# Four edits around the first layer norm of a streaming encoder step: a bank of its own for one block product, subtractions on VectorE, another order of four tiles, and a later start of the gate rows

## The chip, the core and the metric

The kernel runs on one core of one Trainium2 chip. The metric is device time in microseconds (us). It is one program, launched once, and no part of the arithmetic is done on the host.

## The reference, cut to what matters

One layer works on 576 tokens, 512 of a new stream and 64 of a running one, with a model width of 1024. Everything is float32.

```python
h = layer_norm(ALPHA*x + 0.5*swiglu_ffn(x, ffn1_w_gu, ffn1_w_down), ln1_g, ln1_b)
z = h @ w_in        # mLSTM q,k,v,o,i,f | attention q,k,v | two branch gates
h = layer_norm(ALPHA*h + w_out(sig(g_m)*P_m(mLSTM(z)) + sig(g_a)*P_a(BandAttn(z))), ln2_g, ln2_b)
y = layer_norm(ALPHA*h + 0.5*swiglu_ffn(h, ffn2_w_gu, ffn2_w_down), ln3_g, ln3_b)
```

The change lies at the seam between the first two lines: the end of the first feed-forward network (its down projection), the first norm, and the first products with `w_in`. The layer norm takes mean and variance of each token over the 1024 features. The mLSTM's gates i and f (4 heads each) come out of `w_in` too; a cumulative sum and a running maximum over the tokens make decay weights of them.

## The kernel before, in words

**Numbers and tiles.** Activations lie transposed, features on the 128 partitions and tokens along the free dimension, in 8 tiles of 128x576. A float32 product is made of three fast matmuls: each operand is split into a rounded part ("hi", by an ACT copy) and the rest ("lo", by a DVE subtraction, or by an ACT copy with the sign turned and a DMA from POOL's queue that adds the source to it). The three are hi·hi, hi·lo and lo·hi.

**Products in blocks.** The large products use a seven-product scheme on 2x2 blocks (Strassen and Winograd's): one product is 4 tiles of the inner dimension by 3 matmuls, so 12 matmuls of 128x288. The down projection takes its middle third so, in `seven` (L1115), for the output tiles (0,1), (2,3), (4,5) and, last in the first network, (6,7). `X`, `Y`, `Z` are PSUM banks. `X` collects one product after the other, and between them `ln.take` (L590) adds what stands in `X` to the norm's tiles. A matmul that goes on with `X` must wait until `take` has read it. For the last pair, `first` (L1319) is called inside: there the left token half A of tiles 6 and 7 is complete, and `last` (L600) adds its sums and squares.

**The norm.** `last` leads to `stats` (L648): matmuls with a column of ones give mean and mean square, the reciprocal root is a POOL power, `centre` (L713) subtracts the mean from the eight tiles (tiles 6 and 7 on POOL, the others on DVE, by `CP` at L188), `spread` (L721) brings the scales onto all partitions, and `apply` (L727) scales each tile (DVE), adds the bias (ACT), and splits it into hi (ACT) and lo (DVE). Each half of the tokens goes through this by itself. The halves of the norm are 288 tokens, those of the next product 256 and 320. `centre` serves the second norm and the first half of the third as well.

**The first products with `w_in`.** One `gemm` (L331) makes four tiles: attention v, k and q of the first head pair and the gates i and f (weights 48, 40, 32 and "if"). By `WAVE_M` (L316) the first three take the left half together, tile by tile of the normed activation as it comes, then the fourth the left half; then the same for the right half. The "if" tile has both weight parts packed in one array, so it takes 2 matmuls where the others take 3. There are four PSUM banks of this kind, so the right half's tiles wait for the copies that empty the left half's.

**The units.** `un` (L1709) then runs 12 pairs of tiles of `w_in` by the seven-product scheme, unit after unit. `un.load` brings a pair's raw weights; for every unit DVE makes four sums and the lo parts.

**Order of work.** The order on PE is the order in which the code calls; a clock `od.now` counts matmuls, and `later(d, f)` calls `f` once d of its nanoseconds have gone by. The other engines' rows are placed by a scheduler, by readiness and priority; each engine then runs its rows strictly in the order written. `issue_after` only orders: the step is placed no earlier than another. A planner (`plan`, `pump` at L233) lists all weight blocks in order of use; two raw buffers take turns, SP issues the loads, ACT and DVE split. `PIECES` (L177) names blocks that are split in two halves, `ADDED` (L179) those whose lo part a POOL DMA makes. `gate_rows` (L1375) is a chain of some thirty small steps on 4 partitions, most of them on DVE, handed out one per 1900 of the clock from 50000 after `un.run` has begun (L1760).

Of the kernel before, what the change touches and what calls it, by code (L numbers as in the profile page):

```python
# [14 lines left out]
ALU = mybir.AluOpType  # L15
# [7 lines left out]
KT = D // P  # L23
# [22 lines left out]
class Order:  # L46
# [10 lines left out]
    def later(self, dt, fn):  # L57
        self.seq += 1
        heapq.heappush(self.heap, (self.now + dt, self.seq, fn))
# [29 lines left out]
def tile_layer(ctx: ExitStack, tc: tile.TileContext, ins, outs):  # L89
# [64 lines left out]
    def stt(out, a, s, b, op0, op1):  # L154
        return DVE.scalar_tensor_tensor(out=out, in0=a, scalar=s, in1=b, op0=op0, op1=op1)  # L155
# [9 lines left out]
    def blank(out, like, behind=None):  # L165
# [8 lines left out]
    CL = {1: 2, 2: 3}  # L174
    NX, NX_IN = 10, 11
    NH0, NH1 = 1, 6
    PIECES = {("in", 48), ("in", 40), ("in", 32)}  # L177

    ADDED = {("in", c + j) for c in (32, 40, 48) for j in range(2, KT)} | {("in", c) for c in (*range(2, 8), *range(10, 32), *range(56, 72))} \  # L179
        | {("gu2", 1, 1), ("gu2", 2, 0), ("gu2", 2, 1)}  # L180

    HALVED = {("in", c + j) for c in (32, 40) for j in range(3, KT)}
# [2 lines left out]

    EARLY = [("gu2", 0, 0), ("gu2", 0, 1), ("gu2", 1, 0)]
    EARLY1 = [("in", 16), ("in", 17)]
    CP = (6, 7)  # L188
    GR = 1900
    L_MEAN, L_STATS, L_SPREAD, L_SPREAD1 = 300, 1440, 4920, 2600  # L190
    plan = []
# [190 lines left out]
    def plan_ffn(n):  # L382
        for j in range(CL[n]):
            for e in range(2):
                plan.append(((f"gu{n}", j, e), ins[f"w_gu{n}"][e * FT + j]))
        stops.append(len(plan))

        def chunk(j, c):
            k0, nk = DC[c]
            plan.append(((f"dn{n}", j, c), ins[f"w_dn{n}"][j][:, k0 * P:(k0 + nk) * P]))  # L390

        def seven(j, order="uv"):
            for e, x in enumerate("at"):
                plan.append(((f"ds{n}", j, x), ins[f"w_dn{n}"][j + e][:, KT * P:2 * KT * P]))
            for x in order:
                plan.append(((f"ds{n}", j, x), None))

        for j, c in ((1, 0), (3, 0), (1, 2), (3, 2), (5, 0), (5, 2)):
            chunk(j, c)
        for j in (0, 2, 4):  # L400
            seven(j)
            chunk(j, 0)
            chunk(j, 2)
        if n == 1:
            for j in (6, 7):
                chunk(j, 0)
                chunk(j, 2)
            seven(6, "vu")
            chunk(6, 0)
            chunk(6, 2)  # L410
            return
        for r in range(2):
            for j in (6, 7):
                for c in range(3):
                    chunk(j, c)

    def plan_in(cols_):
        for c in cols_:
            plan.append((("in", c), w_in[c]))

    plan_ffn(1)
    plan_in((48, 40, 32))
    plan.append(("if", ins["w_if"]))
    plan_in((16, 17))
    stops.append(len(plan))
    for j in range(1, KT):
# [688 lines left out]
    def seven(n, j, inner, ln, Y=None, first=None):  # L1115

        ids = {}
        at = {"a11": ("a", 512), "a12": ("a", 0), "t0": ("t", 512), "t1": ("t", 0), "q1": ("u", 512), "a22": ("u", 0),
              "q0": ("v", 0)}

        def product(ps, what, xk, start, end=None):
            w_, c0 = at[what]
            for w in "atuv" if first is None else "atvu":
                if w_ not in ids and w not in ids:
                    ids[w] = take((f"ds{n}", j, w))
            wh, wl = parts[ids[w_]]
            for i in range(4):
                ww = slice(c0 + i * P, c0 + (i + 1) * P)
                xh, xl = inner.b[i][xk]
                for w, x in ((wh, xh), (wh, xl), (wl, xh)):  # L1130
                    mm(ps, w[:, ww], x, start and i == 0 and w is wh and x is xh, False, skip_group_check=True)
                od.tick()
            if end:
                done(ids[end])

        X, Z = bank("mm")[:, :HT_], bank("mm")[:, :HT_]
        new = Y is None
        if new:
            Y = bank()[:, :HT_]
        product(X, "a11", "b11", True)  # L1140
        ln.take(j, A, X, ALU.add)
        product(Y, "a12", "b21", new, "a")
        product(X, "t0", "t2", False)
        ln.take(j, B, X, ALU.add)
        if first is None:
            product(Z, "q1", "t1", True)
            ln.take(j + 1, B, Z, ALU.subtract)
        product(X, "q0", "t3", False, "v")
        ln.take(j + 1, B, X, ALU.subtract)
        if first is None:  # L1150
            product(Z, "t1", "b22", False, "t")
        product(X, "a22", "t4", False, "u" if first is None else None)
        ln.take(j + 1, A, X, ALU.subtract)
        if first is not None:
            first()
            product(Z, "q1", "t1", True, "u")
            ln.take(j + 1, B, Z, ALU.subtract)
            product(Z, "t1", "b22", False, "t")
        return Y, Z

# [212 lines left out]
            stt(hs(dst, hf), hs(dst, hf), scol[:, bc:bc + 1], hs(tmp, hf), ALU.add, ALU.add)  # L1373

    def gate_rows():  # L1375
        yield stt(t1, fx, -1.0, fx, ALU.mult, ALU.max)
        yield act(t1, t1, AF.Exp, scale=-1.0)
        yield ts(t2, t1, 2.0, None, ALU.add)
        for a in range(0, T, 144):
            yield DVE.reciprocal(t2[:, a:a + 144], t2[:, a:a + 144])  # L1380
        yield tt(t1, t1, t2, ALU.mult)
        yield tt(t2, t1, t1, ALU.mult)
        yield ts(t3, t2, 1.0 / 15, None, ALU.mult)
        for c in (13, 11, 9, 7, 5, 3):
            yield stt(t3, t3, 1.0 / c, t2, ALU.add, ALU.mult)
        yield stt(t3, t3, 1.0, t1, ALU.add, ALU.mult)
        yield ts(t3, t3, 2.0, None, ALU.mult)
        yield stt(t3, fx, 0.0, t3, ALU.min, ALU.subtract)
        bcum, arow, mt = t2, t1, t3
        for a, b in ((0, NP_), (NP_, T)):  # L1390
            yield DVE.tensor_tensor_scan(out=bcum[:, a:b], data0=z4.to_broadcast([4, b - a]), data1=t3[:, a:b], initial=0.0,
                                         op0=ALU.add, op1=ALU.add)
        yield tt(arow, li, bcum, ALU.subtract)
        yield DVE.tensor_tensor_scan(out=mrow[:, :NP_], data0=z4.to_broadcast([4, NP_]), data1=arow[:, :NP_], initial=0.0,
                                     op0=ALU.add, op1=ALU.max)
        yield DVE.tensor_tensor_scan(out=mrow[:, NP_:], data0=z4.to_broadcast([4, NS]), data1=arow[:, NP_:],
                                     initial=scol[:, 2:3], op0=ALU.add, op1=ALU.max)
        yield tt(mt, bcum, mrow, ALU.add)
        SP.dma_start(outs["m"][:, 0:1], mt[:, NP_ - 1:NP_])
        SP.dma_start(outs["m"][:, 1:2], mt[:, T - 1:T])  # L1400
        for i, (a, b) in enumerate(((0, NP_), (NP_, T))):
            ts(scol[:, 4 + i:5 + i], mrow[:, b - 1:b], -1.0, None, ALU.mult)
            yield act(rows[32:36, a:b], arow[:, a:b], AF.Exp, bias=scol[:, 4 + i:5 + i])

        yield ts(rows[32:36, :], rows[32:36, :], 1.0 / 16, None, ALU.mult)
        yield act(rows[64:68, :], mt, AF.Exp, scale=-1.0)
        yield act(wd[:, 0:64], mrow[:, NP_:], AF.Exp, bias=scol[:, 2:3], scale=-1.0)
        yield act(wd[:, 64:65], mrow[:, T - 1:T], AF.Exp, bias=scol[:, 2:3], scale=-1.0)

        yield act(mr[0:64, :], mw)  # L1410
        yield tt(mr[32:36, :], mw[0:4, :], f(mr[0:4, :]), ALU.subtract)
        yield None
        for b in range(5):
            w = min(P, T - b * P)
            ps = bank()
            transpose(ps[:w, :P], rows[:, b * P:b * P + w], ident)
            yield DVE.tensor_copy(tcol[:w, b, :].rearrange("p (g h) -> p g h", h=4),
                                  ps[:w, :96].rearrange("p (g r) -> p g r", r=32)[:, :, 0:4])
        gdone.append(1)
        yield None  # L1420
# [9 lines left out]
    def out_cb(t, key, j):  # L1430
        def cb(hf, ps):
            with tc.issue_after(k0a[0].ins) if j == 1 and key == "v" else nullcontext():
                act(hs(t, hf), ps)
            if hf == 1:
                SP.dma_start(outs[key][:, j, :], t)
        return cb
# [265 lines left out]
    def keep_g(c, tiles):  # L1702
        for e in range(2):
# [5 lines left out]
    un = Columns([(b + c, b + c + 1) for c, b in pairs],  # L1709
                 [lambda tiles, c=c, fn=KEEP[b]: fn(c, tiles) for c, b in pairs],  # L1710
                 stp, None, cw, combos)
    un.load(0)
    un.load(1)
    for i, key in enumerate(EARLY1):
        later(9000 + 4000 * i, lambda key=key: early(e1, key, EARLY1))
    gemm([[(("in", 48), KT)], [(("in", 40), KT)], [(("in", 32), KT)], [("if", KT)]], H,
         [out_cb(vf0, "v", 0), out_cb(kf0, "k", 0), q0_cb, gate_cb], WAVE_M)
    wst["ahead"] = 2
    for i in range(4):
        combos.last = combos.add(i)  # L1720
# [9 lines left out]
    with tc.tile_pool(name="cx", bufs=1, side="right", reuse_waits="tile") as cx:  # L1730
# [26 lines left out]
            wst["stop"] = stops[0]  # L1757
            pump(2)

        later(50000, lambda: od.bg.append((GR, gate_rows())))  # L1760
        un.run(tail)
    pstack.close()
    opool.append(ostack.enter_context(tc.tile_pool(name="op", bufs=8, reuse_waits="tile")))
# [563 lines left out]
```

## Time and profile before

| | |
|---|---|
| runs, us | 1553.64, 1553.24, 1552.8 |
| median, us | 1553.24 |
| profiled execution, us | 1553.24 |
| its span, first to last instruction, us | 1551.5 |
| outside the span, us | 1.74 |
| PE busy, us | 1530.7 |
| mean granted TensorE clock | 0.998 |

Stretches below are given in us from the span's start. The first network's down projection ends near 394, the four tiles of `w_in` run to 424.7, two more tiles of `w_in` to 437.5, and the units from there to about 575.

In the views, a row of the timeline gives start, duration, engine, source line, operation, output<-input, and how many instructions it merges; in brackets stands how long the engine had been idle before it and which engine and tile ended that. Tiles are named without their numbers: `s` is any tile of the pool "slots" (norm tiles and hi and lo parts among them), `st` a unit's tile, `wr` and `wu` raw weights, `wh` and `wl` their hi and lo parts, `mm` and `aux` PSUM banks. Line 135 is the helper for every matmul, 149 for an ACT copy, 152 and 155 for DVE's two tensor forms.

### The profile page before, as it was taken

What the parts mean: (1) busy time and instruction counts of PE and PEld (TensorE: products, weight loads), DVE (VectorE), ACT (ScalarE), POOL (GpSimd) and SP (SyncE); (2) the same over time, 40 slices, a digit from 0 to 9 for tenths busy, and PEclk for the clock granted to TensorE, in tenths of its full rate; (3) what the DMA queues carried; (4) which work ended last, traced back from release to release, by engine and by line L of the source; (5) the groups of instructions that cost most, each with busy time, mean ns of one, the idle gap of its engine ahead of it and who ended that gap; (6) DMA issues with size and microseconds to landing.
All of it is one profiled execution on the core that took longest, in us unless ns stands there. A gap on an engine that the chain in (4) does not pass through costs nothing.

```text
span 1551.5 us, 29498 instructions
## 1 busy us (share of the span) xinstructions
PE 1530.7 (99%) x11579; PEld 1516.1 (98%) x11579; DVE 1140.2 (73%) x2103; ACT 891.7 (57%) x1700; POOL 234.7 (15%) x437
## 2 busy tenths in 40 slices
PE   9999999999999999999999999999999999999998
PEld 9999999999899999999999999999999999999997
DVE  7877778675988766777586766755776877788756
ACT  7544457442866557777754877753456454457333
POOL 1000000000310015555311222202121000001000
PEclk9999999999999999999999999999999999999999
DMA  9232323533754438687534765642755323226334
GB/s 262 108 109 83 105 86 93 142 108 89 204 150 155 137 130 223 153 204 188 120 137 137 189 145 138 163 144 82 210 141 128 109 82 109 82 72 145 119 113 150
DMA packets 80260, 211.15 MB, mean 136 GB/s; under 512 B 9081, under 2 KB 20985, under 8 KB 80121
## 3 DMA queue, kind: packets, MB, share of 16 engines
q1 hardware_dynamic: 65144, 169.15, 33.3%
q0 software_dynamic: 11808, 34.28, 12.7%
q10 hardware_dynamic: 3168, 5.83, 1.1%
q8 instruction: 91, 1.49, 0.4%
q14 instruction: 49, 0.39, 0.1%
HBM read 172.27 MB, written 21.63 MB: 125 GB/s over the span
## 4 chain that ended last, share of the span: by engine, by line
PE 87%; DVE 4%; ACT 4%; DMA 2%; POOL 1%; issue 1%; SPq 0%; ACTq 0%; DVEq 0%; POOLq 0%
PE mm L135 70%; PE aux L135 15%; PE aux L145 2%; DVE s L152 1%; ACT sc L149 1%; DVE wl L152 1%; DVE sc L1585 1%; DMA s<-in_xT 1%; ACT s L149 1%; DMA G<-in_rbias 1%; ACT wh L149 0%; POOL kh L159 0%; DMA wr<-in_w_gu 0%; ACT wh L872 0%; DVE s L155 0%
## 5 line engine op out<-in xcount | busy, mean ns | idle before, releaser
L135 PE MATMUL mm<-s,wh 128*128 128x288 f32 (+2 forms) x3667 | 752.2, 298 | 6.9 <-DVE s L152 3.1
L135 PEld LDWEIGHTS mm<-s,wh 128*128 128x128 f32 x3667 | 588.0, 189 | 11.4 <-DVE s L152 2.3
L135 PE MATMUL mm<-s,wl 128*128 128x288 f32 (+2 forms) x1806 | 533.1, 295 | 0.0
L135 PEld LDWEIGHTS mm<-s,wl 128*128 128x128 f32 x1806 | 340.0, 188 | 0.0
L149 ACT ACTIVATE wh<-wr 128x1024 fp32r<-128x1024 f32 (+2 forms) x143 | 134.0, 948 | 156.7 <-PE mm L135 91.3
L152 DVE TENSOR_TENSOR wl<-wr,wh 128x1024 fp32r<-128x1024 f32 (+2 forms) x93 | 107.5, 1164 | 49.0 <-ACT wh L149 48.6
L135 PE MATMUL mm<-tx,wh 128*128 128x288 f32 x677 | 140.3, 296 | 0.8 <-DVE tx L152 0.8
L135 PEld LDWEIGHTS mm<-tx,wh 128*128 128x128 f32 x677 | 109.2, 188 | 1.2 <-DVE tx L152 1.0
L152 DVE TENSOR_TENSOR wl<-wt,wh 128x1024 fp32r<-128x1024 f32 x51 | 62.5, 1225 | 55.8 <-ACT wh L872 55.8
L135 PE MATMUL mm<-tx,wl 128*128 128x288 f32 x350 | 103.2, 295 | 0.0
L872 ACT ACTIVATE wh<-wt 128x1024 fp32r<-128x1024 f32 x51 | 54.1, 1060 | 83.1 <-DVE wt L152 83.1
L152 DVE TENSOR_TENSOR wl<-wu,wh 128x1024 fp32r<-128x1024 f32 x63 | 77.1, 1223 | 31.3 <-ACT wh L872 31.3
L872 ACT ACTIVATE wh<-wu 128x1024 fp32r<-128x1024 f32 x63 | 66.7, 1058 | 41.2 <-PE mm L135 34.3
L135 PE MATMUL mm<-tx,ah 128*128 128x288 f32 x416 | 85.4, 297 | 0.4 <-ACT st L149 0.4
L198 POOL DMA_DIRECT2D s<-s x16 | 13.7, 854 | 469.4 <-DVE hb L152 426.7
L149 ACT ACTIVATE h<-h 128x288 f32<-128x288 f32 x78 | 34.0, 436 | 60.9 <-DVE h L152 60.9
L135 PEld LDWEIGHTS mm<-tx,ah 128*128 128x128 f32 x416 | 66.2, 188 | 1.2 <-ACT st L149 0.6
L135 PEld LDWEIGHTS mm<-tx,wl 128*128 128x128 f32 x350 | 65.7, 188 | 0.0
L152 DVE TENSOR_TENSOR ws<-wu 128x1024 f32<-128x1024 f32 (+1 forms) x55 | 64.7, 1176 | 0.0
L152 DVE TENSOR_TENSOR wl<-ws,wh 128x1024 fp32r<-128x1024 f32 x51 | 62.2, 1219 | 3.0 <-ACT wh L872 3.0
L135 PE MATMUL mm<-h,wh 128*128 128x288 f32 (+2 forms) x304 | 62.7, 296 | 0.1
L135 PE MATMUL mm<-tx,al 128*128 128x288 f32 x208 | 61.1, 294 | 0.0
(398 smaller groups left out, 3481.8 us busy)
## 6 DMA issues: line engine op xcount, KB each, us to landing
wu<-in_w_gu SPq DMA_DIRECT2D x78, 512.0 KB, 4.4
wr<-in_w_in SPq DMA_DIRECT2D x48, 512.0 KB, 4.2
wr<-in_w_dn SPq DMA_DIRECT2D x37, 512.0 KB, 3.8
wl<-in_w_in POOLq DMA_DIRECT2D x36, 512.0 KB, 6.3
wu<-in_w_in SPq DMA_DIRECT2D x24, 512.0 KB, 4.5
wr<-in_w_dn SPq DMA_DIRECT2D x19, 384.0 KB, 3.2
s<-s POOLq DMA_DIRECT2D x16, 288.0 KB, 4.4
wu<-in_w_ap SPq DMA_DIRECT2D x8, 512.0 KB, 4.7
```

The lines of the kernel that those rows point to most:

```text
L135: PE.matmul(out, lhsT, rhs, start=start, stop=stop, **kw)
L145: PE.transpose(out, in_, idn)
L149: return ACT.activation(out, in_, func, **kw)
L152: return (eng or DVE).tensor_tensor(out, a, b, op=op)
L198: return POOL.dma_start(lo, src, accum_op=ALU.add)
L872: self.last = ACT.activation(hi, src, AF.Copy)
L1585: DVE.tensor_tensor_reduce(out=out, in0=ps, in1=g, op0=ALU.add, op1=ALU.min, scale=1.0, scalar=3e38, accum_out=acc)
```

## The change

1. In `seven`, for the last pair (6,7) only, the product of `q1` and `t1` (into `Z`) comes before that of `q0` and `t3`, and the last product into `X` (`a22` by `t4`) goes to a bank `R` of its own, which `take` reads separately. The planner's order of the two blocks "v" and "u" goes back to "u", "v".
2. `CP` is empty: `centre` subtracts on DVE alone, in all norms.
3. The `gemm` of four tiles takes v, k, "if" and, as the fourth, q. The block ("in", 32) of q is loaded after "if", is split in one piece, and gets its lo part by a POOL DMA. The first two `un.load` are called 8000 and 10500 after this point on the clock.
4. `gate_rows` is handed out from 30000 on, and its first step is placed after the lo part of the unit that was prepared last.

```diff
-    PIECES = {("in", 48), ("in", 40), ("in", 32)}
+    PIECES = {("in", 48), ("in", 40)}
...
-    ADDED = {("in", c + j) for c in (32, 40, 48) for j in range(2, KT)} | {("in", c) for c in (*range(2, 8), *range(10, 32), *range(56, 72))} \
+    ADDED = {("in", 32)} | {("in", c + j) for c in (32, 40, 48) for j in range(2, KT)} | {("in", c) for c in (*range(2, 8), *range(10, 32), *range(56, 72))} \
...
-    CP = (6, 7)
+    CP = ()
...
-            seven(6, "vu")
+            seven(6)
...
-    plan_in((48, 40, 32))
+    plan_in((48, 40))
     plan.append(("if", ins["w_if"]))
+    plan_in((32,))
...
-            for w in "atuv" if first is None else "atvu":
+            for w in "atuv":
...
-        if first is None:
-            product(Z, "q1", "t1", True)
-            ln.take(j + 1, B, Z, ALU.subtract)
+        product(Z, "q1", "t1", True)
+        ln.take(j + 1, B, Z, ALU.subtract)
         product(X, "q0", "t3", False, "v")
         ln.take(j + 1, B, X, ALU.subtract)
         if first is None:
             product(Z, "t1", "b22", False, "t")
-        product(X, "a22", "t4", False, "u" if first is None else None)
-        ln.take(j + 1, A, X, ALU.subtract)
-        if first is not None:
+            product(X, "a22", "t4", False, "u")
+            ln.take(j + 1, A, X, ALU.subtract)
+        else:
+            R = bank()[:, :HT_]
+            ln.take(j + 1, A, X, ALU.subtract)
+            product(R, "a22", "t4", True, "u")
+            ln.take(j + 1, A, R, ALU.subtract)
             first()
-            product(Z, "q1", "t1", True, "u")
-            ln.take(j + 1, B, Z, ALU.subtract)
             product(Z, "t1", "b22", False, "t")
...
     def gate_rows():
-        yield stt(t1, fx, -1.0, fx, ALU.mult, ALU.max)
+        with tc.issue_after(un.lo.ins):
+            first = stt(t1, fx, -1.0, fx, ALU.mult, ALU.max)
+        yield first
...
-    un.load(0)
-    un.load(1)
+    for i in range(2):
+        later(8000 + 2500 * i, lambda i=i: un.load(i))
...
-    gemm([[(("in", 48), KT)], [(("in", 40), KT)], [(("in", 32), KT)], [("if", KT)]], H,
-         [out_cb(vf0, "v", 0), out_cb(kf0, "k", 0), q0_cb, gate_cb], WAVE_M)
+    gemm([[(("in", 48), KT)], [(("in", 40), KT)], [("if", KT)], [(("in", 32), KT)]], H,
+         [out_cb(vf0, "v", 0), out_cb(kf0, "k", 0), gate_cb, q0_cb], WAVE_M)
...
-        later(50000, lambda: od.bg.append((GR, gate_rows())))
+        later(30000, lambda: od.bg.append((GR, gate_rows())))
```

Three places show how the rows move. First DVE, while PE makes the last products of the pair (6,7). `s_3591` is tile 7 of the norm and `s_3589` tile 6, `mm_4342` is the bank `X`, `mm_4343` is `Z`, `aux_4420` the new bank `R`; `s_430` and `s_431` are the sums and the sums of squares; `wl` rows split weights. Before:

```order
L152 TENSOR_TENSOR s_3589<-s_3589,mm_4342 128x288
L152 TENSOR_TENSOR s_431_3035<-s_431_3035,sq_4427 128x288
L152 TENSOR_TENSOR s_3591<-s_3591,mm_4342 128x288
L152 TENSOR_TENSOR wl_4411<-wr_4351,wh_4410 128x768
L152 TENSOR_TENSOR s_3591<-s_3591,mm_4342 128x288
L152 TENSOR_TENSOR s_430_3034<-s_430_3034,s_3591 128x288
L152 TENSOR_TENSOR s_431_3035<-s_431_3035,sq_4431 128x288
L152 TENSOR_TENSOR s_3591<-s_3591,mm_4343 128x288
```

Now:

```order
L152 TENSOR_TENSOR s_3589<-s_3589,mm_4342 128x288
L152 TENSOR_TENSOR s_431_3035<-s_431_3035,sq_4442 128x288
L152 TENSOR_TENSOR s_3591<-s_3591,mm_4343 128x288
L152 TENSOR_TENSOR s_3591<-s_3591,mm_4342 128x288 x2
L152 TENSOR_TENSOR s_430_3034<-s_430_3034,s_3591 128x288
L152 TENSOR_TENSOR wl_4426<-wr_4351,wh_4425 128x768
L152 TENSOR_TENSOR s_3591<-s_3591,aux_4420 128x288
L152 TENSOR_TENSOR wl_4489<-wr_4395,wh_4488 128x512
L152 TENSOR_TENSOR s_430_3034<-s_430_3034,s_3591 128x288
L152 TENSOR_TENSOR s_431_3035<-s_431_3035,sq_4446 128x288
```

The read of `Z` has moved up, the two reads of `X` stand together, the read of `R` is an added row, and between it and the reads of `X` stand a sum of the right half and the split of a weight block of 768 columns; half a `w_in` block is split ahead of the two sums of the left half.

Second ACT, in the left half of the norm. `s_3042` and `s_3036` are the first two norm tiles (bias rows), `s_4523`, `s_4538` (now `s_4537`, `s_4555`) their hi parts, `sq` a square. Before:

```order
L149 ACTIVATE wh_4503<-wr_4414 128x512 x2
L149 ACTIVATE wh_4549<-wr_4501 128x512 x2
L149 ACTIVATE s_3042<-s_3042,cols 128x288
L149 ACTIVATE s_3036<-s_3036,cols 128x288
L149 ACTIVATE s_4523<-s_3042 128x288
L149 ACTIVATE wh_4679<-wr_4509 128x8x64
L149 ACTIVATE s_3585<-s_3585,cols 128x288
L149 ACTIVATE sq_4589<-s_3589 128x288
L149 ACTIVATE s_4538<-s_3036 128x288
```

Now:

```order
L149 ACTIVATE wh_4496<-wr_4429 128x512 x2
L149 ACTIVATE wh_4545<-wr_4494 128x8x64
L149 ACTIVATE s_3042<-s_3042,cols 128x288
L149 ACTIVATE s_3036<-s_3036,cols 128x288
L149 ACTIVATE sq_4576<-s_3589 128x288
L149 ACTIVATE s_4537<-s_3042 128x288
L149 ACTIVATE wh_4660<-wr_4502 128x1024
L149 ACTIVATE s_4555<-s_3036 128x288
L149 ACTIVATE wl_4661<-wh_4660 128x1024
L149 ACTIVATE s_3585<-s_3585,cols 128x288
```

The block of q (`wr_4501` before, `wr_4502` now) has moved from ahead of the norm's rows to between the hi parts of the first and the second tile, as one row of 1024, and a second row of 1024 (`wl_4661`) is new.

Third DVE, in the second unit (`ws_5229`, now `ws_5230`, are its weight sums); `t_4611`, `t_4612` and `rows` belong to the gate rows. Before:

```order
L152 TENSOR_TENSOR ws_5229<-wu_4672 128x1024
L159 TENSOR_SCALAR t_4611<-rows 4x576
L152 TENSOR_TENSOR wt_5230<-ws_5229,wu_4672 128x512
L1380 RECIPROCAL t_4611<-t_4611 4x144
L152 TENSOR_TENSOR wt_5230<-wt_5230,wu_4672 128x512
L1380 RECIPROCAL t_4611<-t_4611 4x144 x3
L152 TENSOR_TENSOR st_5172<-mm_5187,st_5172 128x288
L152 TENSOR_TENSOR wl_5248<-wt_5230,wh_5247 128x1024
L152 TENSOR_TENSOR rows<-rows,t_4611 4x576
L152 TENSOR_TENSOR t_4611<-rows 4x576
L159 TENSOR_SCALAR t_4612<-t_4611 4x576
L155 SCALAR_TENSOR_TENSOR t_4612<-t_4612,t_4611 4x576 x4
```

Now:

```order
L152 TENSOR_TENSOR ws_5230<-wu_4839 128x1024
L152 TENSOR_TENSOR wt_5231<-ws_5230,wu_4839 128x512
L152 TENSOR_TENSOR wt_5231<-wt_5231,wu_4839 128x512
L152 TENSOR_TENSOR st_5173<-mm_5188,st_5173 128x288
L152 TENSOR_TENSOR wl_5249<-wt_5231,wh_5248 128x1024
L152 TENSOR_TENSOR wl_5280<-ws_5230,wh_5279 128x1024
L155 SCALAR_TENSOR_TENSOR st_5174<-st_5174,mm_5252 128x288
```

The gate rows have left the second unit; the first of them now stands in the fourth unit and the last in the ninth, one or two at a time between the units' own. On SP, the first load of a unit's weights now stands ahead of the load of q's block.

## The prediction

> **What bounds the kernel now.** I read the page first, then the waits of PE, then PE's timeline at each wait, then the other engines' timelines there.
>
> ```profile
> span 1551.5 us, 29498 instructions
> PE 1530.7 (99%) x11579; PEld 1516.1 (98%) x11579; DVE 1140.2 (73%) x2103; ACT 891.7 (57%) x1700; POOL 234.7 (15%) x437
> ```
>
> PE works for 1530.7 of 1551.5 us. The change removes no matmul, so it can only move PE's 20.8 idle us. The waits of PE (total, times, longest) name the candidates:
>
> ```profile
> PE mm L135 <- DVE s L152: 3.3, 5, 1.2
> PE mm L135 <- ACT vf L149: 1.5, 1, 1.5
> PE mm L135 <- DVE st L155: 1.4, 1, 1.4
> PE mm L135 <- ACT st L149: 0.4, 1, 0.4
> ```
>
> They add up to 6.6 us, the most that this change could win here. PE's timeline shows where they lie:
>
> ```profile
> 379.06 0.50 PE L135 MATMUL mm<-s,wh 128*128 128x288 f32 x2 [1.21 <-DVE s L152]
> 381.53 0.50 PE L135 MATMUL mm<-s,wh 128*128 128x288 f32 x2 [0.64 <-DVE s L152]
> ...
> 384.79 1.39 PE L135 MATMUL aux<-onec,s 128*128 128x1 f32 x12
> ...
> 395.91 0.39 PE L135 MATMUL mm<-s,wh 128*128 128x256 f32 x1 [1.07 <-DVE s L152]
> ...
> 407.91 2.08 PE L135 MATMUL mm<-s,wh 128*128 128x256 f32 x16
> 411.52 0.56 PE L135 MATMUL mm<-s,wh 128*128 128x320 f32 x2 [1.53 <-ACT vf L149]
> ...
> 424.69 0.40 PE L135 MATMUL mm<-s,eh 128*128 128x256 f32 x2
> ...
> 451.83 0.53 PE L135 MATMUL mm<-s,wh 128*128 128x288 f32 x2 [1.44 <-DVE st L155]
> ...
> 482.72 0.53 PE L135 MATMUL mm<-tx,ah 128*128 128x288 f32 x2 [0.40 <-ACT st L149]
> ```
>
> 379.06 and 381.53 are the waits for `take` to read `X`; 384.79 is the left half's statistics; 395.91 the first normed tile; 407.91 the fourth tile's left half; 411.52 the right half, waiting for v's bank; 424.69 the end of the four tiles; the last two lie in the units. So the seam is ruled by a chain through DVE and ACT, not by PE. What counts is when that chain delivers.
>
> **Part 1, the own bank.** It removes 1.21 + 0.64 = 1.85 us of waiting. From 381.53 to 384.79 PE made two products, so one takes 1.6. Without the waits, from 377.7 on: `Z`, `X`, `R` and `Z` again, four products, end at 384.1, `R` at 382.5. But the statistics need sums that DVE makes:
>
> ```profile
> 381.73 0.96 DVE L152 TENSOR_TENSOR wl<-wr,wh 128x768 fp32r<-128x768 f32 x1 [0.34 <-ACT wh L149]
> 383.40 0.45 DVE L152 TENSOR_TENSOR s<-s,mm 128x288 f32<-128x288 f32 x1 [0.71 <-PE mm L135]
> ...
> 384.37 0.46 DVE L152 TENSOR_TENSOR s<-s,sq 128x288 f32<-128x288 f32 x1
> 385.56 0.69 DVE L152 TENSOR_TENSOR wl<-wr,wh 128x512 fp32r<-128x512 f32 x1
> ```
>
> In the new order, once `X` is done at 381.1, come two reads of `X` and a sum (3 x 0.45), the split of 768 columns (0.96), the read of `R` (0.45), half a block (0.6 net of overlap), and the two sums (0.9): 385.1, with the first sum at 384.75. Before, the last of these ended at 384.83. PE, ready at 384.1, waits some 0.75 and begins the statistics at 384.85, the old 384.79. So nothing is won yet, and 12 matmuls that used to follow the statistics now precede them: PE gets through what hides the norm (42 matmuls, 5.6 us, with 1.6 of statistics and 0.3 more) at 392.3.
>
> **Part 2, subtractions on DVE.** From the means to the first tile:
>
> ```profile
> 387.55 1.43 DVE L152 TENSOR_TENSOR s<-s,c 128x288 f32<-128x288 f32 x2
> 389.00 0.97 DVE L152 TENSOR_TENSOR s<-s,sq 128x288 f32<-128x288 f32 x1
> 389.89 1.28 DVE L152 TENSOR_TENSOR wl<-wr,wh 128x512 fp32r<-128x512 f32 x2
> 391.09 1.55 DVE L152 TENSOR_TENSOR s<-s,c 128x288 f32<-128x288 f32 x4
> 392.57 0.93 DVE L155 SCALAR_TENSOR_TENSOR s<-s,cols,aux 128x288 f32<-128x288 f32 x2
> ...
> 395.41 0.81 DVE L152 TENSOR_TENSOR s<-s,s 128x288 fp32r<-128x288 f32 x2
> ...
> 399.43 0.68 DVE L152 TENSOR_TENSOR wh<-wr,wh 128x512 fp32r<-128x512 f32 x1
> ```
>
> ```profile
> 386.81 0.41 ACT L149 ACTIVATE c<-aux 128x288 f32<-128x288 f32 x1
> ...
> 388.54 0.43 ACT L149 ACTIVATE sq<-s 128x288 f32<-128x288 f32 x1
> 388.87 1.14 ACT L149 ACTIVATE wh<-wr 128x512 fp32r<-128x512 f32 x2
> ```
>
> ```profile
> 387.68 1.98 POOL L152 TENSOR_TENSOR s<-s,c 128x288 f32<-128x288 f32 x2
> ...
> 395.46 2.46 POOL L159 TENSOR_SCALAR mr<-rows 64x576 fp32r<-64x576 f32 x2
> ```
>
> Four subtractions alone took 1.55, so about 0.37 each; beside POOL's two, two took 1.43 and a sum 0.97 instead of 0.45. POOL's part cost DVE 1.2 us; on DVE the two cost 0.74, a gain of 0.45 a half. The new order spends it: two subtractions from 387.2, a wait until ACT has the square (388.5, one root row ahead of it where three were), the sum, two more, the two half blocks from 389.66 (ACT's pair at 388.87 releases them), four more, and the "if" split (0.68), which stood at 399.43. That gives 392.95 for the first scaling, against 392.57. Then bias, square and hi on ACT: the first lo part ends at 395.8, against the old release at 395.91. So PE, there at 392.3, waits 3.5: the 1.85 is spent. The second and third norm have PE covered by other products; I take 0, with 0.3 either way.
>
> [...] POOL's 2.46 us of `mr` reads SBUF while DVE subtracts at 395.41, and DVE's rows there are not stretched (0.81 for two). [...]
>
> **Part 3, q as the fourth tile.** Its block's load must wait for the raw buffer that the 40 block leaves at 390.9, and ACT reaches the block's row at 395.15, just ahead of the second tile's hi part. Loads of one `w_in` block around there, alone and behind four unit loads (KB, us to landing):
>
> ```profile
> wr<-in_w_in SPq DMA_DIRECT2D x1, 512.0 KB, 3.8
> ...
> wr<-in_w_in SPq DMA_DIRECT2D x1, 512.0 KB, 6.9
> ```
>
> The first unit load was issued here, the start and length of two on SP's queue:
>
> ```profile
> 391.58 1.42 SPq L864 DMA_DIRECT2D wu<-in_w_in  x2
> ```
>
> Now one unit load is in front of it on SP's queue; I take 4.2, nearer the lower, so 395.25: no loss yet, with 2.7 us more at the upper end. ACT then spends 1.04 on hi, and as much on the sign-turned copy (`el` is the same step of another block, `c` the right half's mean, `vf` the copy that empties v's bank):
>
> ```profile
> 402.02 0.39 ACT L149 ACTIVATE c<-aux 128x288 f32<-128x288 f32 x1
> ...
> 405.54 1.04 ACT L149 ACTIVATE el<-eh 128x1024 fp32r<-128x1024 f32 x1
> ...
> 411.11 0.36 ACT L149 ACTIVATE vf<-mm 128x256 f32<-128x256 f32 x1
> ```
>
> So the second tile's lo part comes at 397.1 and PE loses 0.4 there, and as much again twice where ACT's hi parts come late. The right half's mean, which ended at 402.4, stands three ACT rows of about 0.43 later, at 403.7; then all eight subtractions and the seventh tile's lo (9 x 0.37) run ahead of the eighth tile's lo, which ends at 407.45. PE does that tile by 408.4, then q's 24 matmuls (2.9, by 16 in 2.08): 411.3, where before it was at 410.0. One more copy of 1.04 stands ahead of ACT's right half, and one norm row (0.45) less between that and v's copy, so v's bank is emptied at 412.1 instead of 411.47: +0.6. Six matmuls (0.9) later PE needs the "if" bank, behind the copies of k and four more (5 x 0.36): 413.9, another 0.95 of waiting, where before q's bank cost 0.15. Sum of parts 1 to 3 at 424.69: 0.6 + 0.95 - 0.15 = **+1.4** (0 to +4.1). The unit loads are needed only in the units, after the four tiles and two more: hidden.
>
> **Part 4, gate rows.** DVE between 440 and 452:
>
> ```profile
> 440.93 2.85 DVE L1380 RECIPROCAL t<-t 4x144 f32<-4x144 f32 x3
> ...
> 447.19 3.09 DVE L155 SCALAR_TENSOR_TENSOR t<-t,t 4x576 f32<-4x576 f32 x4
> ...
> 451.34 0.43 DVE L155 SCALAR_TENSOR_TENSOR st<-st,mm 128x288 f32<-128x288 f32 x1
> ```
>
> The last row releases PE at 451.83; 5.94 us of gate rows stand in the 11 before it. It needs an ACT copy of a product that ended at 447, so without them it is ready at 448, before PE needs it (450.4). The 0.40 at 482.72 is the same queue. Gone: **-1.84**. In their new place the rows fill DVE's slack of some 3 us in a unit of seven products (11.1); my count has one unit over by 1.3, within the 1.9 that PE allows. I take **+0.2** (0 to 1.3).
>
> Sum: 1.4 - 1.84 + 0.2 = -0.24. The profiled execution took 1553.24, equal to the median, with 1.74 outside its span: **1553.0**.
>
> **The rivals.** (a) *The chain gives way*: scheduled rows run closer, or the sums come as soon as PE is done, so the 1.85 is kept, v's wait (1.53) vanishes behind q's 24 matmuls, and the gate rows' 1.84 with them: 1548.0. For it: all three waits are in the rows; against it: DVE's queue as counted. (b) *Slower, by q's load*: if the unit load in front of it is let go only at the end of the down projection (392.3), SP issues q's block at about 392.7 or later; at 6.9 us it lands at 399.6 and ACT, stopped at 395.15, gives the second tile 4.4 us late: 1557.4. It decides from a landing after 395.2; it is over 0.2% slower from 398.6 on. For it: SP's queue is strict; against it: the buffer of that unit load was free by 391.58 before. (c) *Gate rows were not the cause*: the units' own DVE rows are late, +1.4 stays, 1554.6. [...]
>
> **How the numbers follow.** A measurement of this kernel can tell about 0.2% (3.1 us) from no change. Forecast with its bounds 0.56, (a) 0.15, (b) 0.13, (c) 0.12, (d) 0.04. Faster by over 0.2% (under 1550.1) takes (a): 0.15. Slower (over 1556.3) takes most of (b): 0.11. Within: 0.74. The range reaches down to half of what (a) adds and up past (c), (d) and the load's upper end (1553.0 + 2.7): 1550.3 to 1556.0.
>
> **What would show it.** Right: no wait at the two `X` products; a new wait of about 0.75 at the statistics; 3 us or more before the first `w_in` matmul; the right half starting near 412 with a wait at the "if" bank; 426 for the end of the four tiles; no wait near 452. Wrong: the four tiles end before 424.7, or PE waits over 1 us in the units, or ACT stands at q's block after 396.

## The result, and the profile after

| | before | after |
|---|---|---|
| median of 19 runs, us | 1553.71 | 1555.92 |
| lowest and highest | 1552.39, 1555.94 | 1553.59, 1557.91 |
| ratio after/before | | 1.0015, 95% interval 1.0008 to 1.0021 |
| profiled execution and its span, us | 1553.24, 1551.5 | 1557.87, 1556.2 |
| PE busy, us | 1530.7 | 1537.2 |
| mean granted clock | 0.998 (profiled), 0.998 or 0.999 in 120 later runs | 0.997 or less in 18 of 19 runs |

The change costs 2.2 us, where the forecast was a gain of 0.24. The time lies within the range and within the 0.2% that were called no change, but the interval excludes no change. The profiled execution lies near the upper end of the 19, so its rows show more of the loss than the medians do. One reason lies outside the seam: near its end, from 1529.0 to 1532.75, the clock was down for another 3.42 us.

The page of the kernel after, its first part and the clock by slices:

```profile
span 1556.2 us, 29491 instructions
PE 1537.2 (99%) x11579; PEld 1523.1 (98%) x11579; DVE 1137.7 (73%) x2112; ACT 893.5 (57%) x1701; POOL 226.1 (15%) x428
...
PEclk9999999999899999999999999999999999999999
```

PE is busy 6.5 us longer with the same 11579 matmuls. It doesn't only wait; it works more slowly. The one 8 in the last row is the slice from 389 to 428. The windows there (PE, PEld, DVE, ACT, POOL busy with instructions, then granted clock, DMA share, GB/s) before:

```profile
390.00:394.00 4.00, 4.00 (x30) 3.90 (x29) 4.00 (x9) 2.06 (x6) 0.03 (x1) 1.00 0.53 136
394.00:396.00 2.00, 0.92 (x6) 0.48 (x4) 2.00 (x6) 1.82 (x6) 1.86 (x4) 1.00 0.95 346
396.00:398.00 2.00, 2.00 (x18) 2.00 (x18) 2.00 (x6) 1.23 (x4) 1.88 (x3) 1.00 1.00 381
...
404.00:406.00 2.00, 1.83 (x15) 1.62 (x15) 2.00 (x6) 2.00 (x5) 0.27 (x1) 1.00 0.00 0
```

and after:

```profile
390.00:394.00 4.00, 3.53 (x25) 3.19 (x24) 4.00 (x10) 1.18 (x3) 0.94 (x2) 1.00 0.58 190
394.00:396.00 2.00, 0.29 (x1) 0.19 (x1) 2.00 (x6) 1.63 (x4) 1.78 (x4) 1.00 1.04 361
396.00:398.00 2.00, 1.72 (x8) 1.57 (x7) 1.29 (x4) 1.24 (x2) 0.55 (x2) 0.50 0.96 299
...
404.00:406.00 2.00, 2.00 (x11) 2.00 (x10) 0.73 (x2) 2.00 (x7) 0.00 (x0) 0.50 0.34 64
406.00:408.00 2.00, 2.00 (x16) 1.91 (x15) 1.64 (x5) 2.00 (x5) 0.00 (x0) 0.94 0.00 0
```

From 396.0 to 406.2 the granted clock is 0.50, summed over quarter microseconds for 10.24 us. At half the clock that makes 5.1 us more of PE's busy time, and the 3.42 near the end 1.7. In the 2 us ahead of 396, PE has done 0.29 us of work. PE's timeline after:

```profile
385.39 1.47 PE L135 MATMUL aux<-onec,s 128*128 128x1 f32 x12 [0.38 <-DVE s L152]
...
395.71 0.38 PE L135 MATMUL mm<-s,wh 128*128 128x256 f32 x1 [2.19 <-ACT s L149]
396.37 0.58 PE L135 MATMUL mm<-s,wh 128*128 128x256 f32 x1 [0.28 <-DVE s L152]
...
399.93 2.55 PE L135 MATMUL aux<-onec,s 128*128 128x1 f32 x12
...
415.01 0.56 PE L135 MATMUL mm<-s,wh 128*128 128x320 f32 x2 [0.48 <-ACT vf L149]
416.72 0.85 PE L135 MATMUL mm<-s,wh 128*128 128x320 f32 x4 [0.56 <-ACT t L149]
...
428.85 0.40 PE L135 MATMUL mm<-s,eh 128*128 128x256 f32 x2
```

The two waits at `X` are gone. In their place stands one wait of 2.19 ahead of the hi part of the first normed tile, and 0.28 ahead of its lo part. In the kernel before, PE didn't wait for the hi part, and the 1.07 was for the lo part:

```profile
394.46 0.38 PE L135 MATMUL mm<-s,wh 128*128 128x256 f32 x1
```

After the wait the statistics of the right half, the same twelve matmuls as at 385.39, take 2.55 us, since the clock is halved. To compare stretches I set each profile's zero at DVE's read of an `aux` bank near 373, before and after:

```profile
372.75 0.45 DVE L152 TENSOR_TENSOR s<-s,aux 128x288 f32<-128x288 f32 x1 [3.08 <-PE aux L135]
```

```profile
373.53 0.46 DVE L152 TENSOR_TENSOR s<-s,aux 128x288 f32<-128x288 f32 x1 [2.13 <-PE aux L135]
```

From there to the first `eh` matmul, the end of the four tiles, it was 51.94 us (424.69 - 372.75) and is 55.32: the seam is 3.38 longer. I call this the seam below. In the units the wait of 1.44 is gone.

A second thing shows on SP's and ACT's timelines after: a unit's load goes out ahead of q's block, and ACT stands 1.10 us at that block.

```profile
389.88 0.33 SPq L865 DMA_DIRECT2D wu<-in_w_in  x1
391.52 0.33 SPq L252 DMA_DIRECT2D wr<-in_w_in  x1
```

```profile
396.76 1.06 ACT L149 ACTIVATE wh<-wr 128x1024 fp32r<-128x1024 f32 x1 [1.10 <-DMA wr<-in_w_in]
397.73 0.43 ACT L149 ACTIVATE s<-s 128x288 fp32r<-128x288 f32 x1
```

So there were two theories. **A**: the long wait lets the granted clock fall, and that is the loss. **B**: q's block is late, ACT gives the second tile's hi part (397.73) late, and the rest follows.

### The profile page after: what moved, and what is told of

Read it like the earlier page. It is cut to its first block, busy times and chain, and to the rows that moved or that the text cites. A ratio compares the mean times of both kernels' runs of the same rounds, so it can differ in the third digit from the quotient of the medians.

```text
span 1556.2 us, 29491 instructions
## 1 busy us (share of the span) xinstructions
PE 1537.2 (99%) x11579; PEld 1523.1 (98%) x11579; DVE 1137.7 (73%) x2112; ACT 893.5 (57%) x1701; POOL 226.1 (15%) x428
## 4 chain that ended last, share of the span: by engine, by line
PE 87%; ACT 4%; DVE 4%; DMA 2%; issue 1%; POOL 1%; DVEq 0%; POOLq 0%; ACTq 0%
PE mm L135 70%; PE aux L135 15%; PE aux L145 2%; DMA G<-in_rbias 1%; ACT sc L149 1%; DVE sc L1589 1%; ACT wh L149 1%; ACT wh L873 1%; ACT s L149 1%; DVE wl L152 1%; DMA og<-od 0%; DMA wr<-in_w_in 0%; POOL kh L159 0%; DVE kl L152 0%; DVE ptl L152 0%
```

## The experiments

All times are medians of 11 runs beside the kernel before on the same chip. "Low clock" counts the runs with a mean granted clock of 0.997 or less; the kernel before had 0 of 120 such runs in all. The count is coarse. In the profiles before and after the clock is also down in the last 4.6 and 3.1 us, and one fall of 3.4 us takes only 1.7 off 1551, about 0.001, so a mean of 0.998 doesn't rule one out: the profiles of e9_q_first and e12_part2 have 0.998 and such a fall at the seam. (20 of the 120 runs of the kernel before have 0.998.) The seam's difference is from one profile each.

| run | us | to before, us | ratio, 95% interval | low clock | seam |
|---|---|---|---|---|---|
| e1_fill16 | 1555.20 | +1.21 | 0.9996 to 1.0014 | 7 of 11 | +0.96 |
| e2_no_part1 | 1554.45 | +0.46 | 0.9995 to 1.0013 | 8 of 11 | +1.47 |
| e3_no_part3 | 1556.78 | +2.79 | 1.0008 to 1.0025 | 9 of 11 | +4.28 |
| e4_part4 | 1553.03 | -0.96 | 0.9987 to 1.0005 | 0 of 11 | +0.01 |
| e5_fill512x10 | 1555.21 | +1.33 | 0.9996 to 1.0013 | 5 of 11 | +2.81 |
| e6_fill128x4 | 1555.98 | +2.10 | 1.0000 to 1.0018 | 10 of 11 | +3.41 |
| e7_part1 | 1556.05 | +2.17 | 1.0003 to 1.0021 | 8 of 11 | +2.02 |
| e8_part3 | 1552.15 | -1.73 | 0.9976 to 0.9994 | 0 of 11 | -1.44 |
| e9_q_first | 1554.18 | +0.17 | 0.9992 to 1.0010 | 4 of 11 | +1.48 |
| e10_q_first_fill | 1552.64 | -1.37 | 0.9982 to 1.0000 | 0 of 11 | +0.47 |
| e11_parts34 | 1552.25 | -1.76 | 0.9979 to 0.9996 | 0 of 11 | -1.41 |
| e12_part2 | 1556.06 | +2.05 | 1.0004 to 1.0021 | 4 of 11 | +3.29 |
| e13_part1_fill | 1553.77 | -0.33 | 0.9989 to 1.0007 | 0 of 11 | +0.34 |
| e14_parts134_fill | 1553.34 | -0.76 | 0.9985 to 1.0003 | 0 of 11 | -0.25 |

**e1_fill16**, spare matmuls in PE's wait of the changed kernel:

```diff
 o = pss[t, hf][:, :HALVES[hf][1]]
+for _ in range(fill):     # 16 at the first tile of the four-tile gemm
+    PE.matmul(o[:, 0:P], ones_r, ones_r, start=True, stop=True)
+fill = 0
```

> The changed kernel with 16 spare matmuls of 128 columns (ones by ones, overwritten by the first real one) put into TensorE's wait ahead of the first normed tile's product; they compute nothing of the output. Theory A (the 2.2 us wait lets the granted clock fall to 0.50 for 10.2 us, and that is the loss): the wait shrinks to about 0.5, the clock stays 1.00 from 390 to 410, the right half's statistics take 1.4 again instead of 2.55, mean clock 0.998, time about 1553.6, that is 2.3 below the changed kernel. Theory B (q's block lands late and ACT stands at it, the clock is a by-product): the time stays at 1555.5 to 1556 whatever the clock does.

Neither, cleanly. In the profiled execution the clock stayed up and the statistics took 1.39 again, but 7 of 11 runs still had a low clock. The three runs at 0.999 took 1552.06, 1552.80 and 1553.75; the seven low ones took 1554.91 to 1555.65. In these ten the time goes with the clock, from run to run of one and the same kernel. The eleventh, at 0.998, was the slowest, 1556.98; its cause is open. What brought the clock down was not removed in all of them.

**e2_no_part1, e3_no_part3, e4_part4**: the change without part 1, the change without part 3, and part 4 alone; their code is that of the diff above.

> Parts 2, 3 and 4 without part 1 (the last product in X's bank again). Theory A: the two waits at X are back (1.2 and 0.6), so PE comes later to the first normed tile and waits at most 1.5 in one piece there; the clock stays 1.00, mean 0.998; part 3 costs its 1.4 and part 4 gives 1.6: about 1553.5. Theory B: q's load is as late as before, ACT stands 1.1 at it: 1555.5 with a clock that doesn't fall.

> Parts 1, 2 and 4 without part 3 (q third, split into pieces as before). Theory A: the wait ahead of the first normed tile is still 2 us or more, the clock falls to 0.50 for about 10 us, and the time is 1554.5 (the changed kernel less part 3's 1.4). Theory B: with q's load back in its place nothing is late: 1552.0, the kernel before less part 4's 1.6.

> Part 4 alone on the kernel before. Both theories: the waits of 1.44 and 0.40 in the units go, up to 0.6 comes back: 1552.0 to 1552.5 against 1553.7. If the gate rows were not the cause: 1553.7 and the two waits stay.

Both theories missed e2 and e3. Without part 1 PE still waited 1.51 and 0.58 for the first tile, and that was enough for the clock (0.50 for 3.41 us from 398.25 on). Without part 3 the wait grew to 4.21, the clock fell for 10.24 us, and the time came to 2.79 over before, no less than with part 3: the loss is not part 3's. What part 3 is worth can't be read from this run, since another load is late in it: ACT stands 4.26 us at the "if" block, which is ahead of the first tile's rows. PE's timeline of e3_no_part3, and ACT's:

```profile
396.93 0.91 PE L135 MATMUL mm<-s,wh 128*128 128x256 f32 x2 [4.21 <-ACT s L149]
400.30 2.55 PE L135 MATMUL aux<-onec,s 128*128 128x1 f32 x12
```

```profile
395.16 0.63 ACT L149 ACTIVATE wh<-wr 128x512 fp32r<-128x512 f32 x1 [4.26 <-DMA wr<-in_w_if]
```

Part 4 alone took away both waits in the units (1.84) and left 0.59 in their place; the 0.96 in the medians can't be told from no change by itself.

**e5_fill512x10 and e6_fill128x4**, longer and shorter filling, with the other engines' rows in the same order in both:

```diff
-    PE.matmul(o[:, 0:P], ones_r, ones_r, start=True, stop=True)
+    PE.matmul(pss[t, hf], ones_r, ones_r[:, 0:1].to_broadcast([P, 512]), start=True, stop=True)
```

> The changed kernel with 10 spare matmuls of 512 columns (a column of ones repeated; overwritten by the first real one) in TensorE's wait ahead of the first normed tile; they keep the array's columns busy, where the 16 of 128 columns in the run before covered the wait but filled it only half. [...] Theory B (the fall comes from the later, shorter waits, or the fillers don't count): clock 0.996 in most runs as in e1_fill16, 1555.2.

> Control to e5_fill512x10: 4 spare matmuls of 128 columns (0.4 us) in the same place; VectorE's and ScalarE's rows stand in the very same order as there. Theory A: clock still falls in most runs, 1555.5. [...]

The control stayed at +2.10 with 10 of 11 low, as A says, so the few rows that the fillers move don't help by themselves. The full filling left 5 of 11, which A alone doesn't explain. Its profile does. PE's timeline of e5_fill512x10, and ACT's:

```profile
394.17 2.35 PE L359 MATMUL mm<-ones_r 128*128 128x512 f32 x10
397.17 0.38 PE L135 MATMUL mm<-s,wh 128*128 128x256 f32 x1 [0.28 <-DVE s L152]
399.66 0.88 PE L135 MATMUL mm<-s,wh 128*128 128x256 f32 x2 [1.40 <-ACT s L149]
400.86 2.30 PE L135 MATMUL aux<-onec,s 128*128 128x1 f32 x12
```

```profile
398.22 1.06 ACT L149 ACTIVATE wh<-wr 128x1024 fp32r<-128x1024 f32 x1 [1.33 <-DMA wr<-in_w_in]
```

Behind the filled wait stands a second one of 1.40, for the second tile's hi part, which ACT makes only after q's late block; the clock falls behind that one (0.50 for 6.83 us from 401.1 on). Theory B's late load is real, and it works through the clock too.

**e7_part1 and e8_part3**, single parts:

> Part 1 alone on the kernel before. Theory A: the two waits at X go, their 1.85 us joins the 1.07 ahead of the first normed tile to one wait of 2.5 us or more, the clock falls in most runs (mean 0.996), 1555.5 to 1556. Theory C (the wait is just moved, the clock falls only by what parts 2 and 3 add): 1553.7, clock 0.999.

> Part 3 alone on the kernel before. Theory A: the wait ahead of the first normed tile stays at about 1.1, the clock at 0.999, and the time shows what part 3 costs through DVE's and ACT's chain: the forecast of +1.4 gives 1555.2; the +1.0 of the seam in e1_fill16's profile 1554.8. Theory B (q's load late behind the unit load): ACT stands over 1 us at q's block, 1556 or more.

Part 1 alone costs the whole 2.17, as A has it (a wait of 2.88, the clock at half for 10.24 us). The three of its runs that the count leaves out, at 0.998, took 1555.02 to 1556.05, so the count doesn't catch all of the loss. Part 3 alone is a gain of 1.73, against both theories and against the prediction. On SP, q's block goes out first here (391.36, the unit loads from 391.74), and ACT doesn't stand at it. PE has no wait at the first tile. DVE's timeline says why; in the kernel before, the halves of q's block are split (1.28) between the first scalings and the first lo part:

```profile
392.57 0.93 DVE L155 SCALAR_TENSOR_TENSOR s<-s,cols,aux 128x288 f32<-128x288 f32 x2
393.42 1.28 DVE L152 TENSOR_TENSOR wl<-wr,wh 128x512 fp32r<-128x512 f32 x2
394.62 0.50 DVE L155 SCALAR_TENSOR_TENSOR s<-s,cols,aux 128x288 f32<-128x288 f32 x1
395.05 0.44 DVE L152 TENSOR_TENSOR s<-s,mm 128x288 f32<-128x288 f32 x1
395.41 0.81 DVE L152 TENSOR_TENSOR s<-s,s 128x288 fp32r<-128x288 f32 x2
```

and in e8_part3 only the "if" split (0.68) stands there, with the lo part (394.61) ahead of the read of the bank:

```profile
392.73 0.93 DVE L155 SCALAR_TENSOR_TENSOR s<-s,cols,aux 128x288 f32<-128x288 f32 x2
393.58 0.68 DVE L152 TENSOR_TENSOR wh<-wr,wh 128x512 fp32r<-128x512 f32 x1
394.18 0.51 DVE L155 SCALAR_TENSOR_TENSOR s<-s,cols,aux 128x288 f32<-128x288 f32 x1
394.61 0.45 DVE L152 TENSOR_TENSOR s<-s,s 128x288 fp32r<-128x288 f32 x1
```

The lo part comes 0.98 earlier against the zero of each profile (372.75, 372.93), close to the 1.07 that PE waited. Later ACT copies v's bank at 405.60, ahead of the right half's norm rows, where before it stood behind them at 411.11; so the 1.53 goes as well, and 0.55 and 0.95 of new waits come. ACT's row in e8_part3:

```profile
405.60 0.39 ACT L149 ACTIVATE vf<-mm 128x256 f32<-128x256 f32 x1 [0.41 <-PE mm L135]
```

The seam is 1.44 shorter, and there is a gain in the units too, with the gate rows in their old place. DVE's timeline of e8_part3 there:

```profile
446.51 2.31 DVE L155 SCALAR_TENSOR_TENSOR t<-t,t 4x576 f32<-4x576 f32 x3
448.75 0.43 DVE L155 SCALAR_TENSOR_TENSOR st<-st,mm 128x288 f32<-128x288 f32 x1
```

The unit's row that PE waits for (451.34 in the prediction's rows of before) now stands ahead of one gate row and of a split of 1.2. Of the waits of 1.84 in the units 0.93 is left, as 0.44 and 0.49.

**e9_q_first and e10_q_first_fill**, the unit loads held behind q's load, without and with the ten spare matmuls:

```diff
+    def load_late(i):
+        with tc.issue_after(wst["q"].ins):     # q's block load, recorded in pump
+            un.load(i)
     for i in range(2):
-        later(8000 + 2500 * i, lambda i=i: un.load(i))
+        later(8000 + 2500 * i, lambda i=i: load_late(i))
```

> The changed kernel with one DMA moved: q's block load stands ahead of the first unit load on SP's queue (it stands behind it in the changed kernel); every other row is as there. Theory A (the wait ahead of the first normed tile brings the clock down): q lands before 396, ACT no longer stands at it, which is worth up to 1; the first wait of 2.2 stays, so the clock still falls in most runs: 1555.0 to 1555.5. Theory B (the late load is the loss, through ACT): 1553.5, and a mean clock of 0.998 or more in most runs.

> e5_fill512x10 with the same DMA moved, so neither the first wait nor ACT's stand at q's block is left. Theory A and B together (the five runs of e5_fill512x10 with a low clock had it from the second wait, 1.40 in its profile): clock 0.998 or 0.999 in nearly all runs, 1552.5 to 1553.5. If the clock still falls in half of them, something else brings it down: 1555.

e9_q_first came out nearer to B's 1553.5 than to A's 1555.0: with q's load in time the first wait still brings the clock down, but in 4 of 11 runs by the count and not in most. With e5 and the kernel after these make a square (in the two filled kernels a few rows of DVE and ACT also stand in another order). Both causes in: +2.2, low clock in 18 of 19. Only the late load (e5): +1.33, 5 of 11. Only the long wait (e9): +0.17, 4 of 11, and in its profile the clock is down for 3.42 us instead of 10.24. Neither (e10): -1.37, 0 of 11. The windows of e10_q_first_fill show the clock at full and PE filled:

```profile
394.00:396.00 2.00, 1.72 (x9) 1.01 (x7) 2.00 (x8) 2.00 (x6) 1.88 (x3) 1.00 0.94 340
396.00:398.00 2.00, 1.89 (x12) 1.54 (x13) 1.89 (x6) 2.00 (x4) 0.18 (x2) 1.00 0.95 320
```

Ten matmuls that compute nothing, and one DMA moved, turn a loss of 2.2 into a gain of 1.4 (its interval reaches to no change). Against e10 the late load alone is +2.70, the long wait alone +1.54, both together +3.6. Each does harm without the other; whether they simply add can't be told from medians that are uncertain by about 1.4.

**e11_parts34 and e12_part2:**

> Parts 3 and 4 without 1 and 2. By the runs of the single parts (1552.15 and 1553.03 beside 1553.9) 1551.3, clock 0.998 to 0.999, no wait over 1.3 before 430. If the two gains are one and the same (both just shorten the same seam): 1552.2.

> Part 2 alone on the kernel before. The prediction on record took 0 with 0.3 either way: 1553.9, clock 0.999. Theory A with e2_no_part1's profile, where PE waited 1.51 and 0.58 for the first normed tile: the six subtractions on DVE make that tile later, PE waits over 1.5 there, the clock falls in about half of the runs, 1555.

Parts 3 and 4 give -1.76, no more than part 3 alone. The two gains are in part one and the same, though not in the seam: part 3 alone has already taken 0.91 of the 1.84 in the units, and part 4 beside it brings the waits from 0.93 to 0.6. So little can't be seen in medians that are uncertain by about 1.4. This and e8_part3 are the two fastest kernels here. Part 2, costed at 0 on record, is +2.05. The clock seems to be only some of it: the seven runs at 0.998 and 0.999 average 1555.33, 1.3 over before, though those at 0.998 can hold a fall, and the three at 0.999 average 1554.72, 0.7 over. In the profile the seam is 3.29 longer, and the clock's 3.42 us at half account for at most 1.7 of that. DVE in e12_part2:

```profile
391.63 2.29 DVE L152 TENSOR_TENSOR s<-s,c 128x288 f32<-128x288 f32 x6
393.85 1.28 DVE L152 TENSOR_TENSOR wl<-wr,wh 128x512 fp32r<-128x512 f32 x2
395.05 0.50 DVE L155 SCALAR_TENSOR_TENSOR s<-s,cols,aux 128x288 f32<-128x288 f32 x1
```

With six subtractions in a row, the scheduler puts q's split ahead of the first scaling, which comes 1.6 later than before (395.05 - 373.65 against 392.57 - 372.75).

**e13_part1_fill and e14_parts134_fill:** part 1 with eleven spare matmuls of 512 columns; and parts 1, 3 and 4 with both mends.

> Part 1 alone with 11 spare matmuls of 512 columns in the wait ahead of the first normed tile; no other row differs from e7_part1. If the granted clock is all that part 1 costs, the clock is 0.999 in nearly all runs and the time is the kernel before's, 1553.9 to 1554.0 (the chain delivers no sooner, so nothing is won either). If the moved product costs something by itself (DVE's and ACT's order behind it), the clock is up and the time stays at 1555 or more.

> Parts 1, 3 and 4 without part 2, q's load ahead of the unit loads, the wait filled with 10 spare matmuls of 512 columns. If the chain through VectorE and ScalarE sets when the first tile comes, part 1 adds nothing to parts 3 and 4: 1552.2 with a clock of 0.999. If PE's earlier arrival is worth something once the clock holds: up to 1.85 less, 1550.4.

e13 differs from e7_part1 in the spare matmuls alone, and goes from +2.17 with 8 of 11 low to -0.33 with none. DVE's and ACT's rows stand in the same order in both around the seam, and the first tile's hi part reaches PE 22.87 after the zero of both profiles (395.48 - 372.61, 396.92 - 374.05). PE's timeline and the clock's window of e7_part1, then of e13_part1_fill:

```profile
395.48 0.38 PE L135 MATMUL mm<-s,wh 128*128 128x256 f32 x1 [2.88 <-ACT s L149]
...
398.00:400.00 2.00, 2.00 (x12) 2.00 (x11) 1.13 (x3) 0.53 (x1) 0.00 (x0) 0.50 1.03 420
```

```profile
393.88 2.56 PE L359 MATMUL mm<-ones_r 128*128 128x512 f32 x11
396.92 0.39 PE L135 MATMUL mm<-s,wh 128*128 128x256 f32 x1 [0.47 <-ACT s L149]
...
398.00:400.00 2.00, 1.87 (x17) 1.67 (x15) 2.00 (x6) 1.80 (x5) 0.00 (x0) 1.00 0.94 367
```

So the clock is what part 1 costs; with it held, no gain or loss can be seen (-1.7 to +1.1 by e13's interval). e14, at 1553.34, is over both values that were expected, and no faster than parts 3 and 4 without part 1.

## Why the prediction was wrong, step by step

- **Part 1, the step that failed.** "PE, there at 392.3, waits 3.5: the 1.85 is spent" was the right mechanism: the waits at `X` are gone, PE comes to the first tile early and waits. But the wait was booked at nothing, on the premise that the change "can only move PE's 20.8 idle us". It also lengthened PE's busy time, by 6.5 us in the profile. 1.85 us in two pieces and 1.07 in a third are not the same as one wait (2.88 in e7_part1): behind this one the clock is at half, in that profile for 10.24 us. Booked rightly, part 1 is +2.17 alone, and 0 (-0.33) with the wait filled. The sizes were off too: the wait at the statistics (0.75 forecast) is 0.38, and the 3.5, counted to the first lo part, came as 2.19 for the hi part and 0.28 for the lo part. (The prediction's own terms put the end of DVE's first sum at 384.9, not 384.75; on its scale PE began the statistics at 384.61.)
- **Part 2** was taken at 0, and is +2.05 alone. The count of DVE's rows held for the kernel with all parts (first scaling forecast at 392.95, measured 393.49 - 0.78 = 392.71), where part 3 has taken q's split out of DVE's queue. The share of each part was wrong: what part 2 loses, part 3 gives back in part. In e2_no_part1, with parts 2 and 3, the first scaling is still 0.97 later than before (394.91 - 374.12 against 392.57 - 372.75).
- **Part 3** was +1.4 in the sum, and alone is -1.73. The forecast saw the ACT copies that it adds and not the 1.28 of DVE that it removes ahead of the first tile. Its load was forecast at 4.2 to landing and "no loss yet"; it took 5.2, and ACT stood 1.10. That part of rival (b) came true, by the unit load in front, which was let go early and not late.
- **Parts 1 to 3 together** were to make the seam 1.4 longer. It is 3.38 longer in the profile, 0.96 in that of e1_fill16, where the clock stayed up, and 0.47 in e10_q_first_fill, where q's load is in time as well. So as a sum of queues the forecast was near, but by luck: its terms were wrong by part and cancelled. The missing term was the clock.
- **Part 4** went as forecast in the rows: both waits (1.84) gone, and 0.35 and 0.25 new, where 0.2 was taken. The medians of e4_part4 give -0.96, not resolved. Rival (c) is out. What the forecast didn't see is that part 3 moves a row in the units too, so that the two gains overlap.
- **Rival (d)**, with 0.04 of the chances: no run shows a term for it. In the kernel after, POOL's rows for `mr` took 1.88 from 394.56 on, and DVE's subtraction at 395.13, beside them, took 0.45, no more than the one at 398.18 with POOL idle (0.46).

## What to carry to other kernels

When PE is nearly always busy, price a wait by its length in one piece as well as by the sum: moving several short waits into one can cost more than it saves, by the clock of the matmuls behind it. Here 1.85 and 1.07 became 2.88, the clock behind it was 0.50 for 10.24 us, and the time rose by 2.17 (e7_part1). Read the granted clock in windows of 2 us around the longest wait, and count it over many runs, since one profile may miss it (that of e1_fill16 has 1.00 from 370 to 430, and 7 of its 11 runs were low). To test it, fill the wait with spare matmuls into a bank that is overwritten anyway, and change nothing else (e13_part1_fill: none of 11 runs low, where e7_part1 had 8). Cost the parts of a change singly too: rows that one part adds can stand in the queue just where another part has made room (part 2 is +2.05 alone, where q's split of 1.28 still stands in DVE's queue; part 3 takes it out).

## What the runs showed of the hardware

In windows of 0.25 us the granted clock was 1.00 or 0.50, with values between at the edges of a fall (0.65 from 406.05 on in the kernel after). At the seam it was down for 3.42, 6.83 or 10.24 us, so for about one, two or three times 3.41 (in the profiles of e9_q_first and e12_part2, of e5_fill512x10, and of the kernel after). Why it comes in these lengths, and why the same kernel is caught in some runs and not in others (4 of 11 of e9_q_first), was not shown. In the profiles it came down at the end of gaps of 1.51 and 0.58 (e2_no_part1), of 1.68 and 0.60 (e12_part2), or of 2.18 alone (e9_q_first), while the kernel before, whose profile has 1.07 at the first tile and 1.53 at the right half, had no low clock in 120 runs, by a count that can miss a single fall of 3.4 us.

How much filling keeps the clock up was not settled. Sixteen spare matmuls of 128 columns covered 1.90 us of the wait (1078 columns per us) and left 7 of 11 runs low, ten of 512 columns covered 2.35 (2179 per us) and left 5. Both still had the late load, so it stays open whether the narrow ones count for less.
